# Split operands written as all even tokens and then all odd ones: the order of the writes in a two-layer decoder trunk on one Trainium2 core

## The chip, the cores and the metric

The kernel runs as one program on one core of one Trainium2 chip. A core has four engines that matter here, each with its own instruction queue: PE (TensorE, matrix products), DVE (VectorE), ACT (ScalarE) and POOL (GpSimd). DMA queues move data between the chip's main memory (HBM) and the core's working memory (SBUF); matmuls write into an accumulator memory (PSUM), from which DVE and ACT read. The metric is the time of one execution in microseconds on the device. It was 2062.76 us before the change (median of three runs, 2061.18 to 2065.05).

## The reference: what is computed

Two layers of a decoder trunk for 256 tokens of width 2048, with 16 learned tokens ahead of them (272 in all), everything in float32:

```python
def reference(x, meta_tokens, ...):
    h = jnp.concatenate([meta, x], axis=1)
    for layer in range(DEPTH):                       # 2
        xn = rmsnorm(h, norm_mix[layer])
        if layer < N_A_LAYERS:                       # layer 0: gated linear attention
            h = h + gla_mixer(xn, ...)
        else:                                        # layer 1: windowed attention with sinks
            h = h + swa_mixer(xn, k_sh, v_sh, ...)
        h = h + sq_relu_mlp(rmsnorm(h, norm_mlp[layer]), w_mlp_up[layer], w_mlp_down[layer])
        if layer == N_A_LAYERS - 1:
            k_sh, v_sh = shared_kv(h, kv_norm, w_kv, pos)
    return rmsnorm(h[:, N_META:], norm_final)

def sq_relu_mlp(xn, w_up, w_down):
    return jnp.square(jax.nn.relu(xn @ w_up)) @ w_down
...
```

The MLPs go from 2048 to 8192 and back, and are most of the arithmetic. In the gated attention the mixer's result is scaled by its norm and by `silu(g)` before the output projection; in the windowed attention 32 query heads read 4 shared key and value heads in a band of 128 tokens.

## The kernel before

**Layout.** The stream `h` stays in SBUF, transposed: 16 tiles of 128 rows (the width) by 272 tokens. Every product takes a block of 128 x 128 weights as the stationary operand and streams tokens past it; 16 such blocks are summed in PSUM for one tile of the result. Weights come from HBM in pieces of 512 KB by the queue of SyncE.

**Split operands.** The products are wanted at more precision than PE's fast float32 format (`float32r`) has, so each operand is split into a high part in that format and a low part, the rest. A product is then three matmuls: high weights by high tokens, high weights by low tokens, low weights by high tokens. Weights are split by `split_weight`: ACT makes the high part (L89), DVE the low part (L91). Token operands are kept in the class `Split`: one tile of 2n words for n tokens, in which the order in memory is even tokens' high parts, even tokens' low parts, odd tokens' high parts, odd tokens' low parts. So each part is two rows of n/2 words: 136 for the 272 tokens, 128 for the 256 without the learned ones.

**How matmuls read it.** `x.hi` and `x.lo` are views in the order of the tokens: token 0 from the even row, token 1 from the odd row, token 2 from the even row again. The two neighbours lie n words apart. Where a result for both parts fits into 512 columns of PSUM (256 tokens), one matmul reads both (L114) and a second one reads the high part (L115); for 272 tokens, and where `apart` is false, there are three matmuls (L118, L119, L120).

**Who writes it.** Four places write token operands, each first the high part on ACT and then the low part on DVE, which reads the high part back:

- `split_x` (L161 ACT, L162 DVE): the stream times a norm's gain, 16 tiles each for the gated attention, both MLPs, keys and values, and queries. Beside many of these, POOL adds up the squares for the next norm (`Square.add`).
- the gated output (L700 ACT, L701 DVE): 16 tiles `y` from `gt`, which L697 makes.
- the MLP's hidden tiles (L730 ACT, L731 DVE): 16 tiles in each of 4 blocks of the two layers, 128 in all.
- the windowed attention's outputs, written into the tile `O` straight from PSUM: `values` (L899 ACT, L900 DVE), 8 times, 480 elements for two tiles of 120 + 120 tokens, and `last_values` (L932 ACT, L933 DVE), twice, for the last 16 tokens of a pair of heads.

Their sources are plain: tokens one behind the other. Before the change the producers walk in the order of the tokens. They read neighbours, and write alternately into the two rows, n words apart (256 words in `O`, a tile of its own with rows of 128).

**What sets the order.** Each engine works its own queue in order. In the opening stage the orders of PE, ACT and DVE are written out by hand, and in the windowed attention and its output projection the order of PE is (`manual_schedule`). Everywhere else a planner orders the instructions of each engine when the program is built; it plays the program through with expected durations (L1069):

```python
    with tile.TileContext(nc, schedule_with_timeline_sim=True) as tc:
        trunk(tc, aps, out)
```

**The stages around which the change lies.** (1) The opening, 0 to about 20 us: loads arrive one by one, x is split tile by tile, and the first products run on parts of the weights (L280, L288, L290; their weights are split by L299 and L300). (2) The gated attention, with the masked decays of six levels (L530 to L538), in which every level s works on groups of s tokens of every 2s. (3) The gated output, about 220 to 338 us: `mix` for each of four heads, whose norm is computed by `Square.rstd` (L188 and L189 split the sum of squares, L190 and L191 add it up over the rows on PE, L197 to L204 make the factor), between the products for the gate. (4) The output projection and the first MLP, to about 1135 us. (5) Keys and values, with queries' x split beside it (L796, L806), to about 1160 us. (6) The windowed attention, to about 1330 us: products for the queries with scores (L874), softmax (L829 to L846), transposes (L885 to L887) and values (L896) of earlier steps between them. (7) Its output projection, the second MLP and the last norm (L987 to L995).

Of the kernel before, what the change touches and what calls it, by code (L numbers as in the profile page):

```python
# [11 lines left out]
F32 = mybir.dt.float32  # L12
F32R = mybir.dt.float32r
I32 = mybir.dt.int32
AF = mybir.ActivationFunctionType
ALU = mybir.AluOpType
# [3 lines left out]
P = 128  # L20
# [25 lines left out]
GRP = QH // KVH  # L46
# [18 lines left out]
def trunk(ctx: ExitStack, tc: tile.TileContext, a: dict, out: bass.AP):  # L65
    nc = tc.nc
# [27 lines left out]
    def pairs_of(t):  # L94

        return t.rearrange("p (j a) -> p j a", a=2)

    class Split:


        def __init__(self, tile_, n):
            self.n, self.both = n, tile_[:, :2 * n].rearrange("p (a s j) -> p s j a", a=2, s=2)
            self.hi, self.lo = self.both[:, 0], self.both[:, 1]

    def passes(ps, hi, lo, xs, first, last, m=P, apart=True):

# [50 lines left out]

    def split_x(src, scale_col):
        x = Split(xp.tile([P, 2 * L], F32R, tag="x", name="x"), src.shape[-1])
        src = pairs_of(src)  # L160
        nc.scalar.activation(x.hi, src, AF.Copy, scale=scale_col)  # L161
        nc.vector.scalar_tensor_tensor(x.lo, src, scale_col, x.hi.bitcast(F32), ALU.mult, ALU.subtract)  # L162
        return x

    class Square:
# [57 lines left out]
    with ExitStack() as gla:  # L223
# [41 lines left out]
        def take(k0, k1):  # L265
            for k in range(k0, k1):
                xs.append(split_x(h[k], gains[:, 0, k:k + 1]))
# [54 lines left out]
        with tc.manual_schedule(engines={mybir.EngineType.PE, mybir.EngineType.Activation, mybir.EngineType.DVE}):  # L322
# [3 lines left out]
            for u in range(2):  # L326
                for m in range(NF):
# [4 lines left out]
                    part = m % 2  # L332
# [63 lines left out]
        with tc.issue_after(scaled_keys.ins):  # L396
            for m in range(NF, 8):
                ps, = product(a["w_in"][8 + m], xs, begun=w5 if m == NF else None, pool=aux if m == NF else acc)
# [22 lines left out]
        for m in range(8):  # L421
            log_gate(m)
            ps, = product(a["w_in"][m], xs)
# [11 lines left out]
        with tc.issue_after(rank_done.ins):  # L435
            for li, s in enumerate(LEVELS):
                n = P // (2 * s)
# [246 lines left out]
        for m in range(KT):  # L684
            g, mm = divmod(m, 4)
            if mm == 0:
                mix(g)
            ps, = product(a["w_in"][32 + m], xs)
            gt = tp.tile([P, L], F32, tag="t1", bufs=4, name="gt")
            nc.vector.tensor_mul(gt, ps, rs)  # L690
            sg = tp.tile([P, L], F32, tag="t2", bufs=4, name="sg")
            nc.gpsimd.tensor_scalar_max(sg, gt, -80.0)
            nc.scalar.activation(sg, sg, AF.Exp, scale=-1.0)
            nc.scalar.activation(sg, sg, AF.Ln, bias=1.0)
            nc.scalar.activation(sg, sg, AF.Exp, scale=-1.0)
            nc.vector.tensor_mul(gt, gt, sg)
            nc.vector.scalar_tensor_tensor(gt, OT[g][:, mm], no[:, mm:mm + 1], gt, ALU.mult, ALU.mult)  # L697
            y = Split(yp.tile([P, 2 * L], F32R, tag="y", bufs=KT, name="y"), L)
            gt = pairs_of(gt)
            nc.scalar.copy(y.hi, gt)  # L700
            nc.vector.tensor_sub(y.lo, gt, y.hi.bitcast(F32))  # L701
            ys.append(y)

        xs, sq = [], Square()
# [9 lines left out]
    def mlp(layer, xs, sq, cols, finish):  # L714
        n = cols.stop - cols.start
        rs = sq.rstd(D, "rs", split=True)
        with tc.tile_pool(name="hid", bufs=KT) as hp, tc.tile_pool(name="wp2", bufs=1) as wp2:
            for b in range(NB):
                hs = []
                for m in range(KT):  # L720
                    if b == 0 and m == 4:
                        pools.append(wp2)
                    ps = total(product(a[f"w_up{layer}"][b * KT + m], xs))
                    u = tp.tile([P, L], F32, tag="t1", bufs=4, name="u")[:, :n]
                    nc.vector.scalar_tensor_tensor(u, ps, 0.0, rs, ALU.max, ALU.mult)
                    u2 = tp.tile([P, L], F32, tag="t2", bufs=4, name="u2")[:, :n]
                    nc.scalar.square(u2, u)
                    y = Split(hp.tile([P, 2 * L], F32R, tag="hid", name="hid"), n)
                    u2 = pairs_of(u2)
                    nc.scalar.copy(y.hi, u2)  # L730
                    nc.vector.tensor_sub(y.lo, u2, y.hi.bitcast(F32))  # L731
                    hs.append(y)
                for m in range(KT):
                    ending = layer == 1 and b == NB - 1 and m == KT - 1
                    for term in product(a[f"w_down{layer}"][b * KT + m], hs, apart=not ending):
                        nc.vector.tensor_add(h[m][:, cols], h[m][:, cols], term)
                    if b == NB - 1:
                        finish(m)
            pools.remove(wp2)
# [3 lines left out]
    def to_kv(m):  # L743
        xk.append(split_x(h[m], gains[:, 2, m:m + 1]))
        sq1.add(h[m])

    mlp(0, xs, sq, slice(0, L), to_kv)


    X = slice(NM, L)  # L750
    rs1 = sq1.rstd(D, "rs", split=True)
    with ExitStack() as swa:
# [37 lines left out]
        for i in range(2):  # L790
            for m in range(4):
# [5 lines left out]
                ps = kv[m][:, :L]  # L797
# [4 lines left out]
                else:  # L802
                    t = tp.tile([P, L], F32, tag="t1", bufs=4, name="vt")
# [14 lines left out]
        O = ap.tile([P, KT, 2, 2, SEQ // 2], F32R, name="O")  # L818

        def attended(part, ms, tokens):  # L820

            return O[:, ms, :, part, tokens.start // 2:tokens.stop // 2].rearrange("p m a j -> p m j a")
        N1, N3 = P - NM, NM
        N2 = N1 + P

# [24 lines left out]
        class Step:  # L850
# [39 lines left out]
            def values(self):  # L890
                PT, m0 = self.PT, self.m0
                ps = acc.tile([P, 512], F32, tag="acc", name="ps_pv")
                pv = ps[:, :2 * N2].rearrange("p (i q) -> p i q", i=2)
                for t, q, begin, end in ((0, slice(0, N1), True, True), (1, slice(N1, N2), True, False), (2, slice(N1, N2), False, True)):
                    for par, kv in enumerate(HALVES):
                        nc.tensor.matmul(pv[kv, :, q], VT[t // 2][:, self.pair, kv], PT[t][:, 2 * par:2 * par + 2, :q.stop - q.start], start=begin, stop=end)  # L896
                oh, ol = (attended(part, slice(m0, m0 + 2), slice(0, N2)) for part in range(2))
                pv = pv.rearrange("p i (j a) -> p i j a", a=2)
                nc.scalar.copy(oh, pv)  # L899
                nc.vector.tensor_sub(ol, pv, oh.bitcast(F32))  # L900

# [22 lines left out]
            def last_values(self):  # L924
                ps = aux.tile([P, 512], F32, tag="aux", name="ps_pv3")
                for b, nb in enumerate((P, P, NM)):
                    for t, kv in zip(self.PT3, HALVES):
                        nc.tensor.matmul(ps[kv, :P], VT[b][:nb, self.pair, kv], t[:nb, b], start=(b == 0), stop=(b == 2))
                ms = slice(self.pair * GRP, (self.pair + 1) * GRP)
                src = ps[:, :P].rearrange("p (i j a) -> p i j a", i=GRP, a=2)  # L930
                oh, ol = (attended(part, ms, slice(N2, SEQ)) for part in range(2))
                nc.scalar.copy(oh, src)  # L932
                nc.vector.tensor_sub(ol, src, oh.bitcast(F32))  # L933
# [8 lines left out]
        with tc.manual_schedule(engines={mybir.EngineType.PE}):  # L942
            steps = []
            for t in range(2 * GRP // 2):
                pair, j = divmod(t, GRP // 2)
# [46 lines left out]
    for k0, k1 in ((0, 1), (1, 3), (3, 6), (6, 10), (10, 14), (14, KT)):  # L992
        t = scaled[:, k0:k1]
# [80 lines left out]
```

## Time and profile before

One execution was profiled. Its own time was 2060.31 us, and the profile's span is 2058.6 us.

| | |
|---|---|
| median of three runs | 2062.76 us |
| the three runs | 2061.18, 2062.76, 2065.05 us |
| the profiled execution's own time | 2060.31 us |
| its span | 2058.6 us |
| mean granted clock of PE | 0.997 |
| HBM read over the span | 376.82 MB, 184 GB/s with what is written |

How to read the lines. The page gives for each engine its busy time, its share of the span and its count of instructions. PEld is the loading of weights, which overlaps with PE. A row of a group names the line, the engine, the operation, result and sources, their shapes, the count, the busy time in us and the mean duration in ns; behind the bar stands how long the engine had been idle just before, and what ended most of that. Matmuls are pipelined, so each lasts longer (0.28 us for 272 columns) than the distance to the next one (0.11 us). On ACT and DVE, too, a next instruction can begin shortly before the one ahead has ended, so the distances of starts are what a queue of them costs. A wait is put down to the instruction that released it last.

The page's chain of work that ended last and its costliest groups, apart from those that the prediction shows, in short: splitting weights takes 740.4 us of ACT (L89, 707 times, 1048 ns) and 872.4 us of DVE (L91, 707 times, 1235 ns); the matmuls of the two MLPs, L114, L115 and L118 to L120, are nearly all of PE.

### The profile page before, as it was taken

How to read it: one execution, taken by the hardware profiler on the slowest of the kernel's cores; microseconds unless marked ns; L12 is line 12 of the kernel's file. 1: busy time of each engine (PE TensorE's matmuls, PEld its weight loads, DVE VectorE, ACT ScalarE, POOL GpSimd, SP SyncE). 2: the span in 40 equal slices, each digit the busy share in tenths (PEclk: the TensorE clock that was granted, in tenths of full speed). 3: DMA queues.
4: the chain of work that ended last, by engine and by line, in shares of the span. 5: the costliest groups of instructions: out<-in, count | busy, mean ns of one | idle time of the engine just before them, and what ended most of it. 6: DMA issues, size and time to landing. Idle time of an engine off the chain costs nothing. (4 is left out here: it accounts for less than half of the span.)

```text
span 2058.6 us, 39099 instructions
## 1 busy us (share of the span) xinstructions
PE 2030.5 (99%) x15978; PEld 1951.3 (95%) x15978; DVE 1404.8 (68%) x1999; ACT 1130.7 (55%) x1729; POOL 202.3 (10%) x209
## 2 busy tenths in 40 slices
PE   9999999999999999999999999999999999999997
PEld 9999999999999999999999988999999999999997
DVE  7799677766556556655667777697666666666776
ACT  7565665455345435534554578756546545644653
POOL 0000233300000000000024111060000000000032
PEclk9999999999999999999999999999999999999999
DMA  7644445565655555555554654466666666666662
GB/s 242 194 160 142 150 144 180 189 230 190 192 188 191 189 192 187 192 188 193 186 190 154 203 161 141 135 229 211 203 199 203 200 201 202 201 200 203 200 200 103
DMA packets 109124, 383.85 MB, mean 186 GB/s; under 512 B 13328, under 2 KB 15888, under 8 KB 108944
## 3 DMA queue, kind: packets, MB, share of 16 engines
q1 hardware_dynamic: 106640, 378.29, 56.9%
q0 software_dynamic: 1152, 2.38, 0.4%
q8 instruction: 125, 2.05, 0.4%
q10 hardware_dynamic: 1152, 0.68, 0.1%
q14 instruction: 55, 0.45, 0.1%
HBM read 376.82 MB, written 2.10 MB: 184 GB/s over the span
## 5 line engine op out<-in xcount | busy, mean ns | idle before, releaser
L91 DVE TENSOR_TENSOR lo<-raw,hi 128x1024 fp32r<-128x1024 f32 x707 | 872.4, 1235 | 468.8 <-ACT hi L89 460.8
L89 ACT CAST hi<-raw 128x1024 fp32r<-128x1024 f32 x707 | 740.4, 1048 | 782.4 <-PE ps L119 435.8
L119 PE MATMUL ps<-x,hi 128*128 128x272 f32 (+1 forms) x2032 | 567.4, 279 | 2.3 <-DVE x L162 2.3
L118 PE MATMUL ps<-x,hi 128*128 128x272 f32 (+1 forms) x2032 | 568.6, 280 | 0.0
L120 PE MATMUL ps<-x,lo 128*128 128x272 f32 (+1 forms) x2032 | 567.6, 280 | 0.3 <-DVE lo L91 0.3
L119 PEld LDWEIGHTS ps<-x,hi 128*128 128x128 f32 x2032 | 385.5, 190 | 2.9 <-DVE x L162 2.7
L118 PEld LDWEIGHTS ps<-x,hi 128*128 128x128 f32 x2032 | 385.5, 190 | 2.6 <-issue 2.1
L120 PEld LDWEIGHTS ps<-x,lo 128*128 128x128 f32 x2032 | 385.3, 190 | 1.1 <-DVE lo L91 0.6
L114 PE MATMUL ps<-x,hi 128*128 128x512 f32 x1024 | 335.9, 382 | 0.0
L114 PE MATMUL ps<-hid,hi 128*128 128x512 f32 x1008 | 330.1, 382 | 0.0
L118 PE MATMUL ps<-hid,hi 128*128 128x272 f32 (+1 forms) x1040 | 290.1, 279 | 0.0
L119 PE MATMUL ps<-hid,hi 128*128 128x272 f32 (+1 forms) x1040 | 290.1, 279 | 0.0
L120 PE MATMUL ps<-hid,lo 128*128 128x272 f32 (+1 forms) x1040 | 290.1, 279 | 0.0
L115 PE MATMUL ps<-x,lo 128*128 128x256 f32 x1024 | 279.2, 273 | 0.0
L115 PE MATMUL ps<-hid,lo 128*128 128x256 f32 x1008 | 274.1, 273 | 0.0
L114 PEld LDWEIGHTS ps<-x,hi 128*128 128x128 f32 x1024 | 193.5, 189 | 27.0 <-DVE x L162 0.2
L114 PEld LDWEIGHTS ps<-hid,hi 128*128 128x128 f32 x1008 | 190.2, 189 | 26.4
L115 PEld LDWEIGHTS ps<-x,lo 128*128 128x128 f32 x1024 | 196.6, 192 | 0.3 <-DVE lo L91 0.3
L118 PEld LDWEIGHTS ps<-hid,hi 128*128 128x128 f32 x1040 | 196.6, 189 | 0.0
L119 PEld LDWEIGHTS ps<-hid,hi 128*128 128x128 f32 x1040 | 196.6, 189 | 0.0
L120 PEld LDWEIGHTS ps<-hid,lo 128*128 128x128 f32 x1040 | 196.6, 189 | 0.0
L115 PEld LDWEIGHTS ps<-hid,lo 128*128 128x128 f32 x1008 | 193.5, 192 | 0.2
(259 smaller groups left out, 2214.0 us busy)
## 6 DMA issues: line engine op xcount, KB each, us to landing
raw<-in_w_up SPq DMA_DIRECT2D x256, 512.0 KB, 4.2
raw<-in_w_down SPq DMA_DIRECT2D x256, 512.0 KB, 4.2
raw<-in_w_in SPq DMA_DIRECT2D x91, 512.0 KB, 3.4
raw<-in_w_out_a SPq DMA_DIRECT2D x32, 512.0 KB, 4.0
raw<-in_w_q SPq DMA_DIRECT2D x32, 512.0 KB, 3.6
raw<-in_w_out_b SPq DMA_DIRECT2D x32, 512.0 KB, 3.4
raw<-in_w_kv SPq DMA_DIRECT2D x8, 512.0 KB, 3.5
sw<-qt POOLq DMA_DIRECT2D x32, 64.0 KB, 4.3
```

The lines of the kernel that those rows point to most:

```text
L89: nc.scalar.copy(hi, raw)
L91: nc.vector.tensor_sub(lo, raw, hi.bitcast(F32))
L114: nc.tensor.matmul(both, wh, x.both, start=begin, stop=False)
L115: nc.tensor.matmul(both[:, 1], wl, x.hi, start=False, stop=end)
L118: nc.tensor.matmul(out, wh, x.hi, start=begin, stop=False)
L119: nc.tensor.matmul(out, wh, x.lo, start=False, stop=False)
L120: nc.tensor.matmul(out, wl, x.hi, start=False, stop=end)
```

## The change

The producers visit the elements in another order: all even tokens, then all odd ones. Each then writes its part as two rows without a gap (136 or 128 words; 120 in `values`, 8 in `last_values`), and reads its source at every second element. `Split` gets two more views, `hi_runs` and `lo_runs`, with the tokens' parity outside; a new helper `runs_of` gives the source in the same order. The low part's read of the high part goes along the same rows. The views `hi`, `lo` and `both`, which the matmuls use, and the tile's layout stay as they were. The weights' splitting is not touched.

```diff
+    def runs_of(t):
+
+        return t.rearrange("p (j a) -> p a j", a=2)
...
         def __init__(self, tile_, n):
             self.n, self.both = n, tile_[:, :2 * n].rearrange("p (a s j) -> p s j a", a=2, s=2)
             self.hi, self.lo = self.both[:, 0], self.both[:, 1]
+            runs = tile_[:, :2 * n].rearrange("p (a s j) -> p s a j", a=2, s=2)
+            self.hi_runs, self.lo_runs = runs[:, 0], runs[:, 1]
...
     def split_x(src, scale_col):
         x = Split(xp.tile([P, 2 * L], F32R, tag="x", name="x"), src.shape[-1])
-        src = pairs_of(src)
-        nc.scalar.activation(x.hi, src, AF.Copy, scale=scale_col)
-        nc.vector.scalar_tensor_tensor(x.lo, src, scale_col, x.hi.bitcast(F32), ALU.mult, ALU.subtract)
+        src = runs_of(src)
+        nc.scalar.activation(x.hi_runs, src, AF.Copy, scale=scale_col)
+        nc.vector.scalar_tensor_tensor(x.lo_runs, src, scale_col, x.hi_runs.bitcast(F32), ALU.mult, ALU.subtract)
...
-            gt = pairs_of(gt)
-            nc.scalar.copy(y.hi, gt)
-            nc.vector.tensor_sub(y.lo, gt, y.hi.bitcast(F32))
+            gt = runs_of(gt)
+            nc.scalar.copy(y.hi_runs, gt)
+            nc.vector.tensor_sub(y.lo_runs, gt, y.hi_runs.bitcast(F32))
...
-                    u2 = pairs_of(u2)
-                    nc.scalar.copy(y.hi, u2)
-                    nc.vector.tensor_sub(y.lo, u2, y.hi.bitcast(F32))
+                    u2 = runs_of(u2)
+                    nc.scalar.copy(y.hi_runs, u2)
+                    nc.vector.tensor_sub(y.lo_runs, u2, y.hi_runs.bitcast(F32))
...
         def attended(part, ms, tokens):
 
-            return O[:, ms, :, part, tokens.start // 2:tokens.stop // 2].rearrange("p m a j -> p m j a")
+            return O[:, ms, :, part, tokens.start // 2:tokens.stop // 2]
...
-                pv = pv.rearrange("p i (j a) -> p i j a", a=2)
+                pv = pv.rearrange("p i (j a) -> p i a j", a=2)
                 nc.scalar.copy(oh, pv)
                 nc.vector.tensor_sub(ol, pv, oh.bitcast(F32))
...
-                src = ps[:, :P].rearrange("p (i j a) -> p i j a", i=GRP, a=2)
+                src = ps[:, :P].rearrange("p (i j a) -> p i a j", i=GRP, a=2)
```

## The prediction, made before the changed kernel was run

> **What bounds the kernel now.** I read the page first, then busy time in stretches of 20 us, then the waits of PE.
>
> ```profile
> span 2058.6 us, 39099 instructions
> PE 2030.5 (99%) x15978; PEld 1951.3 (95%) x15978; DVE 1404.8 (68%) x1999; ACT 1130.7 (55%) x1729; POOL 202.3 (10%) x209
> ```
>
> PE is busy for 2030.5 of 2058.6 us. DVE and ACT, on which the whole change lies, have room in the mean, so their own time is worth nothing except where PE waits for them. Does their writing slow PE down in another way, as when both use the memory at once? Two stretches of the first MLP answer that: one of the up projection, where split operands are written, and one of the down projection, where none is.
>
> ```profile
> 600.00:620.00 20.00, 20.00 (x175) 20.00 (x174) 12.53 (x16) 11.41 (x15) 0.00 (x0) 1.00 0.59 187
> 720.00:740.00 20.00, 20.00 (x175) 20.00 (x174) 10.20 (x11) 7.75 (x8) 0.00 (x0) 1.00 0.55 185
> ```
>
> Both hold 175 matmuls. The writes cost PE nothing there, so the 128 pairs of L730 and L731, the greatest part of the change, can bring nothing to the end. What is left is PE's waits:
>
> ```profile
> PE ps_ssq L190 <- ACT sqh L188: 3.7, 2, 1.9
> PE ps L119 <- DVE x L162: 2.3, 2, 1.3
> PE ps_pv L896 <- ACT PT L887: 1.7, 2, 1.5
> PE s L874 <- DVE O L933: 1.4, 1, 1.4
> PE ps L119 <- DVE y L701: 0.9, 1, 0.9
> PE pt L885 <- DVE mx L829: 0.8, 1, 0.8
> PE ps L118 <- ACT y L700: 0.6, 1, 0.6
> PE ps_pv L928 <- ACT PT L920: 0.6, 1, 0.6
> ```
>
> These add up to 12.0 us, and that is all that faster producers could reach, but for one thing: after some waits PE's clock falls. The last three numbers of these rows are granted clock, DMA share and GB/s.
>
> ```profile
> 280.00:300.00 20.00, 20.00 (x155) 19.83 (x155) 14.95 (x25) 11.81 (x20) 6.22 (x3) 0.92 0.50 160
> 300.00:320.00 20.00, 18.26 (x156) 18.00 (x156) 14.05 (x24) 12.61 (x27) 6.96 (x6) 1.00 0.42 134
> 1220.00:1240.00 20.00, 18.29 (x146) 15.60 (x144) 14.04 (x40) 16.54 (x51) 3.87 (x8) 0.91 0.39 123
> ```
>
> 0.08 and 0.09 of 20 us are 1.6 and 1.8 us lost: a dip of the clock costs about 1.7 us, and this execution has two. The first follows the longest wait (L190, 1.9 us), the second the wait at L896 (1.5). The other wait at L190 (3.7 less 1.9, so 1.8 us, in the stretch from 300) is followed by none. So a wait of this size may or may not bring a dip.
>
> **What each producer costs, before and after.** The change alters no count and no destination: the same 15978 matmuls read the same addresses. Only the order in which ACT and DVE visit the elements changes. Now the writes jump by n words at every element; afterwards they run on, and one source is read at every second word.
>
> ```profile
> L730 ACT CAST hid<-u 128x272 fp32r<-128x272 f32 x64 | 43.8, 685 | 2.0
> L188 ACT CAST sqh<-ssq 128x272 fp32r<-128x272 f32 x6 | 2.5, 417 | 3.4 <-POOL ssq L179 3.4
> L161 ACT ACTIVATE x<-h,gains 128x272 fp32r<-128x272 f32 x48 | 35.5, 775 | 1.4 <-DMA gains<-in_gains 0.6 <-DMA h<-in_h 0.5 <-DVE h L151 0.3
> L988 ACT ACTIVATE scaled<-h,gains 128x256 f32<-128x256 f32 x16 | 8.2, 510 | 2.7 <-DVE h L736 2.5
> L731 DVE TENSOR_TENSOR hid<-u,hid 128x272 fp32r<-128x272 f32 x64 | 40.2, 630 | 0.0
> L189 DVE TENSOR_TENSOR sql<-ssq,sqh 128x272 fp32r<-128x272 f32 x6 | 2.6, 438 | 1.7 <-ACT sqh L188 1.7
> ```
>
> L188 and L189 do what L730 and L731 do, with everything in line: 417 for 685 ns on ACT, 438 for 630 on DVE. For L161 the like is L988, 510 for 775. What does a read at every second word cost? The gated attention has it: the last level of L532 and of L535 (s=1) takes every second element.
>
> ```profile
> L535 DVE TENSOR_TENSOR W<-E,K x12: 678/691/705, 114.0 to 188.5; 128x512 f32<-128x512 f32 x12
> L532 ACT ACTIVATE E<-E x12: 629/634/707, 113.0 to 185.5; 128x512 f32<-128x512 f32 x12
> ```
>
> No L535 is above 705 ns (median 691), although at s=1 all its three operands step by two: at most 14 ns on DVE. On ACT the dearest is 73 ns above the median for 512 elements, 39 for 272. So I take **0.19 us** saved on DVE (630 - 438) and **0.22** on ACT (685 - 417 - 39, rounded down; the same for L161). The bounds are 0 (the step is as dear as the jump) and 0.19 and 0.27. [...]
>
> The attention's outputs come from PSUM, and no row reads PSUM at a step.
>
> ```profile
> L899 ACT CAST O<-ps_pv 128x480 fp32r<-128x480 f32 x8 | 8.2, 1028 | 0.9 <-PE ps_pv L896 0.9
> L900 DVE TENSOR_TENSOR O<-ps_pv,O 128x480 fp32r<-128x480 f32 x8 | 8.2, 1027 | 0.9 <-ACT O L899 0.9
> L887 ACT COPY PT<-pt 128x512 f32<-128x512 f32 x24 | 12.7, 585 | 0.0
> L515 DVE TENSOR_TENSOR AT<-ps_d,ident 128x512 f32<-128x512 f32 x2 | 1.4, 692 | 0.0
> ```
>
> With everything in line they would fall to about 0.58 and 0.67; with a step as dear as the jump they stay at 1.03. The nearest row is the instruction itself (same source, same size, one stream out of line), so I take **nothing** saved here and keep 0.44 (ACT) and 0.36 (DVE) for the range. [...]
>
> **Where that reaches PE.** In the gated output stage:
>
> ```profile
> 277.43 0.66 ACT L700 CAST y<-gt 128x272 fp32r<-128x272 f32 x1 [1.51 <-DVE gt L697]
> 277.90 0.42 ACT L188 CAST sqh<-ssq 128x272 fp32r<-128x272 f32 x1
> 335.58 0.66 ACT L700 CAST y<-gt 128x272 fp32r<-128x272 f32 x1 [1.85 <-DVE gt L697]
> 336.27 0.64 DVE L701 TENSOR_TENSOR y<-gt,y 128x272 fp32r<-128x272 f32 x1 [0.72 <-ACT y L700]
> 336.97 0.38 PE L119 MATMUL ps<-y,hi 128*128 128x272 f32 x1
> ```
>
> L188, for which PE waits, stands right behind an L700 on ACT; 0.22 off L700 is 0.22 off the wait, and the second such wait has the same order with one L89 between: 0.44. Then the last y: PE waits for L700 and next for L701, 0.22 + 0.19 = 0.41. Together **0.85**. Behind these waits stand the norm's POOL sums and L697, unchanged, so no more comes out.
>
> In the K/V stage the last x come late on DVE:
>
> ```profile
> 1156.42 1.16 DVE L162 SCALAR_TENSOR_TENSOR x<-h,qgains,x 128x256 fp32r<-128x256 f32 x2
> 1157.41 1.22 DVE L91 TENSOR_TENSOR lo<-raw,hi 128x1024 fp32r<-128x1024 f32 x1
> 1158.55 0.66 DVE L162 SCALAR_TENSOR_TENSOR x<-h,qgains,x 128x256 fp32r<-128x256 f32 x1
> 1159.26 0.38 PE L119 MATMUL ps<-x,hi 128*128 128x256 f32 x1 [1.02 <-DVE x L162]
> ```
>
> Three L162 lie in this line before PE starts again: 3 x 0.19 = **0.57**. DVE's start there is set by a DMA for the rotation, which does not move. At the start of the program:
>
> ```profile
> PEld ps L288 <- DVE lo L300: 0.3, 1, 0.3
> ```
>
> Up to four L162 stand before that L300; I take **0.2** of the 0.3 (0 if a load is late next).
>
> In the attention five L900 lie on the chain; the first and the last:
>
> ```profile
> 1216.04 0.95 DVE O L900
> 1301.94 0.94 DVE O L900
> ```
>
> If they fell by 0.36 each, one would be taken off the wait at L896 and one off that at L928 (0.72), one and the small L933 behind it off that at L874 (0.46), and the last two with an L899 ahead would take away the whole 0.8 at L885: 2.0. With nothing saved on them, it is 0, which I take.
>
> **Sum:** 0.85 + 0.57 + 0.2 = 1.6 us, with both dips as they are. The profiled run took 2060.31 us (1.7 around its span); it becomes 2058.7. It lies 2.45 below the median of the three runs, 2062.76, which becomes **2061.2**; the own range of this case is 2060.2 to 2062.8. A measurement of this kernel can tell about 0.2%, 4.1 us, from no change; so I expect no change that can be told.
>
> **Rivals.** (a) A dip goes: a wait that now brings one is shortened by 0.2 us and stays below what brings it. 1.6 + 1.7 = 3.3, 2059.5; both gone, 5.0, 2057.8. For it: a wait of 1.8 us brought none. Against: 0.2 is little. (b) PSUM at a step is cheap: 1.6 + 2.0 = 3.6, 2059.2, and with a dip gone too 2057.5. For it: L535. Against: PSUM is another memory. (c) The step costs what the jump did and the change moves nothing: 2062.8. Against: L535 and L532. (d) The other side: outside the hand-written stretches a planner orders the work by durations that it expects, and shorter producers may make it choose another order, one in which PE meets a norm's matmul (as L190) before its sum is there. Each such wait costs 1.9 us and a dip of 1.7, 3.6; one gives 2064.8, two give 2068.4, and two are needed for a slowdown that can be told. For it: L190's two waits show that the present order has such places. Against: the attention's PE order is written by hand, and in the MLPs, most of the span, any order keeps PE full.
>
> **Chances.** The forecast 0.35; (a) with one dip 0.22, with both 0.08; (b) 0.20, half of it with a dip; (c) 0.06; (d) 0.09, of which 0.07 beyond 4.1 us. Below 2058.6 are (a) with both dips, (b) with a dip, and 0.04 for scatter of the rest: faster 0.22. Slower 0.07. Same 0.71. The range leaves out the lowest of (a) and (b) and the second step of (d): 2056.5 to 2065.0.
>
> **What would show it.** L730 near 0.46 us and L731 near 0.44; L161 near 0.55; L162 without POOL beside it 0.19 shorter; DVE's and ACT's busy time lower by tens of us with PE's the same; the waits L190, L119 at x and y shorter by 0.2 to 0.6. L899 and L900 at 1.03 confirm the choice, at 0.6 and 0.7 rival (b). Stretches with the clock below 1.00 count the dips. I am wrong if L731 stays at 0.63, or if PE waits at places where it does not now.

## The result and the profile after

| | before | after |
|---|---|---|
| median | 2063.91 us (4 runs, 2061.18 to 2065.08: the three from before and one more) | 2049.73 us (4 runs, 2049.36 to 2050.28) |
| profiled execution | 2060.31 us, span 2058.6 | 2049.36 us, span 2047.6 |

The ratio is 0.9933, with a 95% interval from 0.9916 to 0.9951: about 14 us (10 to 17) off. A second series gave 2050.24 us (5 runs) and 0.9941 [0.9929, 0.9953], about 12 us off. The prediction, 2061.2 us in a range from 2056.5 to 2065.0, missed it.

Every engine issues the same instructions in the same order as before, so all of it is timing. The lines of the changed kernel that matter here lie 6 further down: L118 to L120 are L124 to L126 now, L161 and L162 are L167 and L168, L188 and L190 are L194 and L196, L690 to L701 are L696 to L707, L730 and L731 are L736 and L737, L896 to L900 are L902 to L906, and L933 is L939. All experiments but one (named there) have the changed kernel's line numbers.

The page of the kernel after, its span and busy times:

```profile
span 2047.6 us, 39099 instructions
PE 2025.3 (99%) x15978; PEld 1948.6 (95%) x15978; DVE 1367.4 (67%) x1999; ACT 1088.2 (53%) x1729; POOL 193.7 (9%) x209
```

DVE is busy 37.4 us less and ACT 42.5, "lower by tens of us" as the prediction had it. But the span fell by 11.0 us, and POOL, none of whose instructions was touched, is busy 8.6 us less; 5.3 of these are the maximum over `gt` (L692, 26.7 us before, 21.4 after). The groups of instructions, with shapes kept apart:

```profile
L736 ACT CAST hid<-u 128x256 fp32r<-128x256 f32 x64 | 33.0, 518 | 2.0
L737 DVE TENSOR_TENSOR hid<-u,hid 128x256 fp32r<-128x256 f32 x64 | 30.7, 481 | 0.0
L736 ACT CAST hid<-u 128x272 fp32r<-128x272 f32 x64 | 29.0, 454 | 2.0
L737 DVE TENSOR_TENSOR hid<-u,hid 128x272 fp32r<-128x272 f32 x64 | 27.7, 434 | 0.0
L906 DVE TENSOR_TENSOR O<-ps_pv,O 128x480 fp32r<-128x480 f32 x8 | 5.2, 650 | 0.0
L905 ACT CAST O<-ps_pv 128x480 fp32r<-128x480 f32 x8 | 4.5, 558 | 1.4 <-PE ps_pv L902 1.4
```

For 272 tokens L736 fell from 685 to 454 ns and L737 from 630 to 434: 0.23 and 0.20 us, near the prediction's 0.22 and 0.19. The two reads of PSUM, for which it took nothing, fell from 1028 to 558 and from 1027 to 650. What PE waits for in the kernel after:

```profile
PE ps_ssq L196 <- ACT sqh L194: 1.3, 1, 1.3
PE s L880 <- DVE O L939: 1.0, 1, 1.0
PE ps L125 <- DVE x L168: 0.9, 1, 0.9
PE ps_pv L902 <- ACT PT L893: 0.8, 1, 0.8
PE s L912 <- POOL qs L871: 0.7, 1, 0.7
PE ps L125 <- DVE y L707: 0.7, 1, 0.7
PE ps_pv L934 <- ACT PT L926: 0.6, 1, 0.6
PE ps L124 <- ACT y L706: 0.5, 1, 0.5
```

One of two waits for `sqh` is gone (3.7 us in all became 1.3), one of two for `x` (2.3 to 0.9), one of two for `PT` (1.7 to 0.8). And busy time in stretches of 20 us, where the last three numbers are granted clock, DMA share and GB/s:

```profile
260.00:280.00 20.00, 20.00 (x168) 19.78 (x167) 15.30 (x25) 14.73 (x30) 5.03 (x6) 1.00 0.52 167
280.00:300.00 20.00, 20.00 (x167) 19.78 (x167) 13.28 (x22) 11.64 (x25) 7.00 (x5) 1.00 0.52 177
300.00:320.00 20.00, 18.67 (x161) 18.47 (x160) 15.86 (x27) 10.92 (x20) 6.09 (x5) 1.00 0.40 132
1220.00:1240.00 20.00, 19.30 (x168) 16.69 (x167) 14.20 (x43) 16.36 (x50) 2.53 (x6) 1.00 0.42 136
```

The stretch from 280 us holds 167 matmuls at clock 1.00; before it held 155 at 0.92. Neither of the two dips of the clock is left. Stage by stage (bounds are starts of the same instructions, of keys and values from the first copy of a key tile on; PE's standing time and the loss to the clock are summed over stretches of 0.5 us):

| stage | before | after | PE stands | lost to the clock |
|---|---|---|---|---|
| opening and gated attention | 219.9 | 219.9 | 3.8, 3.8 | 0, 0 |
| gated output | 118.4 | 112.8 | 5.9, 2.6 | 1.7, 0 |
| output projection, first MLP | 806.2 | 805.4 | 0, 0 | 0, 0 |
| keys and values | 16.1 | 14.9 | 2.4, 0.9 | 0, 0 |
| windowed attention | 166.0 | 163.0 | 4.7, 3.2 | 1.7, 0 |
| rest | 732.0 | 731.6 | 11.6, 11.6 | (only behind PE's last work) |

So of 11.0 us, about 6 are standing time, 3.4 the two dips, and some 1.6 lie in differences too small to place.

### The profile page after: what moved, and what is told of

It is laid out like the page before. It is cut to its first block, busy times and chain, and to the rows that moved or that the text cites. A ratio compares the mean times of both kernels' runs of the same rounds, so it can differ in the third digit from the quotient of the medians.

```text
span 2047.6 us, 39099 instructions
## 1 busy us (share of the span) xinstructions
PE 2025.3 (99%) x15978; PEld 1948.6 (95%) x15978; DVE 1367.4 (67%) x1999; ACT 1088.2 (53%) x1729; POOL 193.7 (9%) x209
## 3 DMA queue, kind: packets, MB, share of 16 engines
q0 software_dynamic: 1152, 2.38, 0.4%
## 5 line engine op out<-in xcount | busy, mean ns | idle before, releaser
L91 DVE TENSOR_TENSOR lo<-raw,hi 128x1024 fp32r<-128x1024 f32 x707 | 872.6, 1235 | 502.6 <-ACT hi L89 495.4
L124 PE MATMUL ps<-x,hi 128*128 128x272 f32 (+1 forms) x2032 | 567.8, 279 | 0.0
L126 PE MATMUL ps<-x,lo 128*128 128x272 f32 (+1 forms) x2032 | 566.7, 279 | 0.0
L124 PEld LDWEIGHTS ps<-x,hi 128*128 128x128 f32 x2032 | 384.8, 189 | 2.5 <-issue 2.3
L126 PEld LDWEIGHTS ps<-x,lo 128*128 128x128 f32 x2032 | 384.6, 189 | 0.5
L120 PE MATMUL ps<-x,hi 128*128 128x512 f32 x1024 | 335.7, 382 | 0.0
L120 PE MATMUL ps<-hid,hi 128*128 128x512 f32 x1008 | 330.1, 382 | 0.0
L124 PE MATMUL ps<-hid,hi 128*128 128x272 f32 (+1 forms) x1040 | 290.1, 279 | 0.0
L126 PE MATMUL ps<-hid,lo 128*128 128x272 f32 (+1 forms) x1040 | 290.1, 279 | 0.0
L120 PEld LDWEIGHTS ps<-x,hi 128*128 128x128 f32 x1024 | 193.5, 189 | 27.0
L120 PEld LDWEIGHTS ps<-hid,hi 128*128 128x128 f32 x1008 | 190.2, 189 | 26.3
L124 PEld LDWEIGHTS ps<-hid,hi 128*128 128x128 f32 x1040 | 196.6, 189 | 0.0
L126 PEld LDWEIGHTS ps<-hid,lo 128*128 128x128 f32 x1040 | 196.6, 189 | 0.0
```

What stands on the lines that cost most here:

```text
L91: nc.vector.tensor_sub(lo, raw, hi.bitcast(F32))
L120: nc.tensor.matmul(both, wh, x.both, start=begin, stop=False)
L124: nc.tensor.matmul(out, wh, x.hi, start=begin, stop=False)
L126: nc.tensor.matmul(out, wl, x.hi, start=False, stop=end)
```

## The experiments

Unless said otherwise, a ratio is to the kernel before run on the same chip, whose medians were 2061.9 to 2062.8 us.

### Which producer brings it

Four kernels are the kernel before with one of the four kinds of producer in runs and the others in pairs, for example for the gated output:

```diff
-            gt = pairs_of(gt)
-            nc.scalar.copy(y.hi, gt)
-            nc.vector.tensor_sub(y.lo, gt, y.hi.bitcast(F32))
+            gt = runs_of(gt)
+            nc.scalar.copy(y.hi_runs, gt)
+            nc.vector.tensor_sub(y.lo_runs, gt, y.hi_runs.bitcast(F32))
```

> Only the gated output (ACT hi and DVE lo of y) is written in runs; everything else as before. Theory (the gain comes by stage: in the gated output the shorter producers take away the wait for the sum of squares, POOL's collisions and the clock's dip behind it): the stretch from the first ps_o matmul to the first residual add, 118.5 us before and 112.9 after the whole change, becomes 112.9 to 114; everything else within 0.5 us; total 4 to 6 us below the kernel before. Rival (the gain comes from the mass of producers, the 128 hidden tiles, by less contention everywhere): total within 1 us of before. Rival (only the direct chain counts, as in the prediction): 0.85 us.

> Only split_x is written in runs. Theory: the stretch from the first residual add to the first copy of a query tile, 822.3 us before and 820.3 after, becomes about 820.5, because PE's two waits for x in the K/V stage (2.3 us) fall to 0.9 or less; the attention behind it may shift by a dip of the clock (1.7 us) either way; total 1.5 to 3.5 us below before. Rival (mass of producers): under 1 us.

> Only the attention's outputs O are written in runs, read from PSUM at every second element. Theory: ACT's copy falls from 1028 to about 558 ns and DVE's subtraction from 1027 to about 650, and the stretch from the first query copy to the last ps_pv matmul, 165.9 us before and 162.9 after, becomes 162 to 164; total 2 to 4 us below before. Rival (mass): under 0.5 us. Rival (the dip of the clock alone is what the attention gained, by luck of phase): the waits of PE keep their 4.5 us and only the stretch with clock 0.5 goes.

> Only the 128 hidden tiles of the MLPs are written in runs, which is most of what the change frees on ACT (some 25 us) and DVE (some 21 us). Theory (PE hides them all): total within 0.5 us of before, apart from dips of the clock elsewhere. Rival (mass of producers, contention): most of the 11 to 14 us.

| in runs | median | ratio | to before (2062.7) | stage that changes |
|---|---|---|---|---|
| gated output `y` | 2056.97 | 0.9971 [0.9958, 0.9983] | -5.7 | gated output 112.9 |
| `x` | 2059.78 | 0.9987 [0.9978, 0.9996] | -2.9 | keys and values 15.0 |
| `O` | 2060.06 | 0.9985 [0.9975, 0.9994] | -2.6 | windowed attention 164.8 |
| hidden tiles | 2062.22 | 0.9998 [0.9989, 1.0008] | -0.5 | none |

The four add up to 11.7 us, near the whole. In the profiles the stage of `y` fell by 5.5 us, near its 5.7 (a dip of 1.7 us in the profile of before is among them); the stages of `x` and `O` fell by 1.1 and 1.2 us, less than the 2.9 and 2.6 of the medians, and where the rest of these lies was not found. The 128 hidden tiles, the greatest part of the change, bring nothing that can be told, while 16 tiles of `y` bring nearly half.

### The gated output: VectorE's part or ScalarE's

The kernel before, with only one of the two instructions that write `y` in runs (`runs` and `pairs` are the two views of `gt`):

```diff
-            nc.scalar.copy(y.hi, gt)
-            nc.vector.tensor_sub(y.lo, gt, y.hi.bitcast(F32))
+            nc.scalar.copy(y.hi, pairs)
+            nc.vector.tensor_sub(y.lo_runs, runs, y.hi_runs.bitcast(F32))
```

and the other way round.

> Before, with only VectorE's part of the gated tiles' split (the difference into y) written in runs; ScalarE's copy keeps its pairs. Theory A (a shorter VectorE instruction leaves gaps in which POOL's maximum over gt is not held up): the gated stage falls from 118.4 us to 113 to 114.5 us, PE's longest wait for sqh from 1.9 to 1.3 us or less, time 2057 to 2059 us. Rival B (ScalarE's queue is what was late, and its shorter copy is what helped): the stage stays at 117 to 118.5 us, the time at 2062 to 2064 us.

> Before, with only ScalarE's part of the gated tiles' split (the copy into y) written in runs; VectorE's difference keeps its pairs. Theory A: the gated stage stays at 117 to 118.5 us and POOL's maximum keeps its median of 1.8 us; 2062 to 2064 us. Rival B: the stage falls to 113 to 114.5 us and the time to 2057 to 2059 us, with POOL's maximum as slow as before.

VectorE's part alone: 2059.61 us, 0.9989 [0.9981, 0.9998]. ScalarE's alone: 2062.47 us, 1.0002 [0.9993, 1.0011]. The groups of POOL's maximum, in the kernel before, with VectorE's part and then with ScalarE's:

```profile
L692 POOL TENSOR_SCALAR sg<-gt 128x272 f32<-128x272 f32 x16 | 26.7, 1667 | 65.9 <-DVE gt L690 65.9
```

```profile
L698 POOL TENSOR_SCALAR sg<-gt 128x272 f32<-128x272 f32 x16 | 24.2, 1512 | 65.5 <-DVE gt L696 65.5
```

```profile
L698 POOL TENSOR_SCALAR sg<-gt 128x272 f32<-128x272 f32 x16 | 27.1, 1693 | 65.4 <-DVE gt L696 65.4
```

The rival falls: ScalarE's shorter copy alone brings nothing, and its POOL time is near that of before. Theory A holds in kind but not in size: VectorE's part alone brought 3.1 us, the stage came to 115.5 us, not to 113 to 114.5, and the time lies above the 2057 to 2059 of the theory; one wait for `sqh` went, the other stayed, longer (2.9 us). Only both parts together bring the 5.7.

### What POOL has to do with it

POOL's maximum over `gt` (L692 before, L698 after) stands in the chain of every gate: VectorE makes `gt`, POOL takes the maximum with -80, ScalarE three functions, VectorE two products, ScalarE the copy into `y`. The view of that line, in the kernel before:

```profile
L692 POOL TENSOR_SCALAR sg<-gt x16: 887/1789/2634, 226.9 to 329.7; 128x272 f32<-128x272 f32 x16
...
  ACT sg L693: 23.0, 13
```

and of the kernel after:

```profile
L698 POOL TENSOR_SCALAR sg<-gt x16: 885/1040/2559, 226.8 to 324.4; 128x272 f32<-128x272 f32 x16
...
  ACT sg L699: 14.9, 10
```

These are the least, the median and the greatest duration in ns, and what ScalarE waited for it. The same instruction takes mostly 0.89 to 1.07, 1.79 or about 2.6 us; before the change 5 of the 16 are short (1.07 us or less), after it 10. The timeline of one that changed, before:

```profile
242.34 0.49 DVE L697 SCALAR_TENSOR_TENSOR gt<-OT,norm_out,gt 128x272 f32<-128x272 f32 x1
242.50 2.63 POOL L692 TENSOR_SCALAR sg<-gt 128x272 f32<-128x272 f32 x1 [3.84 <-DVE gt L690]
242.75 1.22 DVE L91 TENSOR_TENSOR lo<-raw,hi 128x1024 fp32r<-128x1024 f32 x1
243.88 0.63 DVE L701 TENSOR_TENSOR y<-gt,y 128x272 fp32r<-128x272 f32 x1
245.16 0.43 ACT L693 ACTIVATE sg<-sg 128x272 f32<-128x272 f32 x1 [1.40 <-POOL sg L692]
```

and after:

```profile
242.04 0.49 DVE L703 SCALAR_TENSOR_TENSOR gt<-OT,norm_out,gt 128x272 f32<-128x272 f32 x1
242.21 1.07 POOL L698 TENSOR_SCALAR sg<-gt 128x272 f32<-128x272 f32 x1 [3.62 <-DVE gt L696]
242.48 1.40 DVE L91 TENSOR_TENSOR lo<-raw,hi 128x1024 fp32r<-128x1024 f32 x1
243.31 0.43 ACT L699 ACTIVATE sg<-sg 128x272 f32<-128x272 f32 x1
243.81 0.43 DVE L707 TENSOR_TENSOR y<-gt,y 128x272 fp32r<-128x272 f32 x1
```

Before, POOL's 2.63 us are the 0.89 of the shortest of the 16 and 1.74 more, and the two VectorE instructions beside it, one right behind the other, last from 242.75 to 244.51, which is 1.76. After, POOL gets through first, and L91 is the one that is held up (1.40 instead of 1.22). So the maximum and VectorE's instructions hold each other up here, POOL by 1.74 us in the first trace and L91 by 0.18 in the second; by what means, no trace shows. In both traces POOL started first, 0.25 and 0.27 us ahead of L91, while L697 (L703 after) was still running; what decided this pair was not found.

For most of the others the order of the starts decides. In the two profiles L91 had started 0.16 to 0.18 us ahead of the maximum 14 times, and these took 1.79 to 2.21 us; in 6 cases L91 started after it and no VectorE instruction ran at its start, and these took 0.89. Four maxima passed from the first kind to the second, such as this one, before and after:

```profile
252.37 1.22 DVE L91 TENSOR_TENSOR lo<-raw,hi 128x1024 fp32r<-128x1024 f32 x1
252.55 1.79 POOL L692 TENSOR_SCALAR sg<-gt 128x272 f32<-128x272 f32 x1 [2.98 <-DVE gt L690]
```

```profile
250.74 0.89 POOL L698 TENSOR_SCALAR sg<-gt 128x272 f32<-128x272 f32 x1 [3.04 <-DVE gt L696]
251.17 1.23 DVE L91 TENSOR_TENSOR lo<-raw,hi 128x1024 fp32r<-128x1024 f32 x1 [0.52 <-ACT hi L89]
```

In all four, L91 came right behind L690 before the change, and after it had to wait (0.17 to 0.52 us) for ScalarE's `hi`, so that POOL was ahead: VectorE, done sooner with the earlier work, had reached L690 before ScalarE had that `hi` ready. It fits that ScalarE's shorter copy alone brought nothing: it lets `hi` come sooner, too.

That the gain lies here and not in VectorE's and ScalarE's own shorter time shows gate by gate, from one start of L690 (L696) to the next. In the five steps whose maximum became shorter by 0.9 us or more (5.2 us together) the step lost 4.5 us, one dip of the clock among them; in the ten others, where the writes became shorter as much, it lost 0.8 in all.

To test it, the maximum goes to VectorE, in the kernel before (no other edit) and in the kernel after:

```diff
-            nc.gpsimd.tensor_scalar_max(sg, gt, -80.0)
+            nc.vector.tensor_scalar_max(sg, gt, -80.0)
```

The planner then moves a few instructions of this stage on PE, VectorE and ScalarE, so here the order is not quite the same.

> Before, all writes in pairs, with the maximum of gt with -80 on VectorE in place of POOL; the planner then moves a few instructions of the gated stage on PE, VectorE and ScalarE. Theory A (POOL's 0.9 to 2.6 us in the chain of the gate are what PE's wait for sqh came from): the gated stage falls from 118.4 us to 111 to 114 us, without a stretch at half clock in it, and the time to 2056 to 2059 us. Rival B (POOL has slack): the stage stays within 1 us of 118.4, the time at 2062 to 2065 us, since VectorE does 16 instructions more.

> After, with the maximum of gt with -80 on VectorE in place of POOL. Theory A: what is left of the wait for sqh (1.3 us once) falls under 0.7 us, the gated stage from 112.8 to 111 to 112 us, the time to 2047.5 to 2049 us. Rival B: within 0.7 us of the changed kernel's 2049.7 us; if VectorE becomes what is late in the stage, 2050 to 2052 us.

The kernel before with it: 2053.84 us, 0.9962 [0.9949, 0.9974]. The kernel after with it: 2047.07 us, 0.9928 [0.9915, 0.9942]. In both the gated output takes 106.5 us and PE does not stand in it at all (2 to 3 us come back in the stages up to the queries). The group in the kernel before with the edit:

```profile
L698 DVE TENSOR_SCALAR sg<-gt 128x272 f32<-128x272 f32 x16 | 4.8, 298 | 0.2
```

0.30 us on VectorE replace 0.89 to 2.63 on POOL. Theory A holds, by more than it had said: without one write in another order, this edit brings 9 us (5 to 11 by the interval). Part of that is the shorter instruction itself, and part may be the planner's other order; the runs do not separate them. Then the other way, the maximum twice on POOL in the kernel after:

```diff
             nc.gpsimd.tensor_scalar_max(sg, gt, -80.0)
+            nc.gpsimd.tensor_scalar_max(sg, sg, -80.0)
```

> After, with the maximum of gt with -80 taken twice on POOL (the second in place, the result unchanged). Theory (the POOL instruction stands in the chain that PE waits for, and stretches at half clock follow PE's waits): the gated stage grows from 112.8 to 115 to 120 us, PE's waits for sqh from 1.3 to 3 to 6 us, time 2052.5 to 2058 us, and the mean granted clock of the runs falls from 0.998 to 0.996 to 0.997. Rival (POOL has slack after the change, the gain came from VectorE's and ScalarE's own time): 2049.7 us within 0.7 us, clock 0.998.

It took 2053.42 us (2052.50 to 2055.06), 3.2 to 3.7 above the kernel after's two medians (other series). Two rows of its waits and groups:

```profile
PE ps_ssq L196 <- ACT sqh L194: 3.6, 2, 2.2
```

```profile
L698 POOL TENSOR_SCALAR sg<-gt 128x272 f32<-128x272 f32 x16 | 20.9, 1304 | 52.3 <-DVE gt L696 45.0 <-ACT hi L89 7.3
L698 POOL TENSOR_SCALAR sg<-sg 128x272 f32<-128x272 f32 x16 | 20.2, 1261 | 1.3
```

The stage grew to 116.0 us and the second wait for `sqh` came back, as the theory said. The clock hardly followed: 0.997 in three of six runs and 0.998 in the others, where 0.996 to 0.997 was expected.

### Keys and values

The kernel before, with the splits of `x` in runs only for 256 tokens (queries and second MLP), or only for 272:

```diff
-        src = pairs_of(src)
+        xh, xl, src = (x.hi_runs, x.lo_runs, runs_of(src)) if src.shape[-1] < L else (x.hi, x.lo, pairs_of(src))
```

> Before, with only the 256-token splits of x (for the queries of attention, and for the second MLP) written in runs. Theory (the splits that stand among the K/V stage's work on ScalarE and VectorE delay the weight splits, the rotation's multiply and so the x that PE waits for): the K/V stage falls from 16.1 us to about 15.0 us, VectorE's wait for the rotation's DMA from 1.8 to about 1.0 us, PE's waits for x from 2.3 to about 0.9 us, time 2059 to 2061 us. Rival (the 272-token splits at the end of the first MLP are late): all of it stays as before, 2062 to 2064 us.

> Before, with only the 272-token splits of x (opening, end of the gated stage, end of the first MLP) written in runs. Theory: K/V stage at 16.1 us, PE's waits for x at 2.3 us, time 2062 to 2064 us. Rival: K/V stage about 15.0 us, waits for x about 0.9 us, 2059 to 2061 us.

For 256 tokens: 2059.95 us, 0.9986 [0.9977, 0.9995], PE's waits for `x` 1.4 us, the stage 15.6 us. For 272: 2061.44 us, 0.9997 [0.9988, 1.0006], waits 2.3 us, the stage 16.2. So it is the splits among the stage's own work that count. For the queries' 256 tokens VectorE's L162 fell from 754 to 485 ns with the whole change, 0.27 us and not 0.19. But the 256-token ones alone did not bring VectorE's wait for the rotation to 1.0 us; it was 1.6. The timeline's row for it, before and after the whole change:

```profile
1155.78 0.72 DVE L775 TENSOR_TENSOR sw<-sw,sin 128x544 f32<-128x544 f32 x1 [1.79 <-DMA sw<-kt]
```

```profile
1148.55 0.73 DVE L781 TENSOR_TENSOR sw<-sw,sin 128x544 f32<-128x544 f32 x1 [0.91 <-DMA sw<-kt]
```

From issue to landing these DMAs took 6.5 us before, 5.0 after, 4.7 with all of `x` in runs, 6.0 and 6.6 with 256 and 272 tokens alone. So a transfer that no edit touches became shorter. Why, is open: they go by POOL's queue (q0 on the page, 2.38 MB), not by the weights' (q1), and no run changed what else goes on at the time.

### The attention's reads of PSUM

The kernel before, with only ScalarE's copies into `O` in runs, or only VectorE's differences:

```diff
-                nc.vector.tensor_sub(ol, pv, oh.bitcast(F32))
+                nc.vector.tensor_sub(*(t.rearrange("p m a j -> p m j a") for t in (ol, pv, oh.bitcast(F32))))
```

> Before, with only ScalarE's copies from PSUM into O in runs; VectorE's differences keep their pairs. Theory A (ScalarE's copy, 1028 to about 560 ns, stands ahead of the probabilities that PE's second matmuls wait for): PE's wait for them falls from 1.5 to about 0.8 us, the wait for O (VectorE) stays at 1.4 us, time 2060.5 to 2062 us. Theory B (VectorE's difference, 1027 to about 650 ns, is the one that counts): no wait but that for O changes, 2062 to 2063.5 us.

> Before, with only VectorE's differences from PSUM into O in runs; ScalarE's copies keep their pairs. Theory A: the wait for the probabilities stays at 1.5 us, the wait for O falls from 1.4 to about 1.0 us, time 2061.5 to 2063 us. Theory B: both waits fall as in the changed kernel, 2059.5 to 2061 us.

ScalarE's part: 2061.37 us, 0.9996 [0.9986, 1.0005]. VectorE's: 2060.00 us, 0.9989 [0.9980, 0.9998]. PE's waits with ScalarE's part, then with VectorE's:

```profile
PE ps_pv L902 <- ACT PT L893: 1.8, 2, 1.5
PE s L880 <- DVE O L939: 1.4, 1, 1.4
```

```profile
PE s L880 <- DVE O L939: 1.0, 1, 1.0
PE ps_pv L902 <- ACT PT L893: 1.4, 1, 1.4
```

Neither theory holds as put. The wait for `O` is VectorE's, as theory A said. The wait for `PT` did not fall with ScalarE's copies, as A wanted, and hardly with VectorE's, as B wanted. With all of `O` in runs it was 0.8 us, but in the profile of the kernel after from the second series it was 1.5 again (0.8 in the first), so it differs between executions of one kernel and decides nothing here. By the times, VectorE's part brings most; how the rest of the stage's 3.0 us divides is open.

### Rows at another distance

L736 and L737 are dearer for 256 tokens than for 272 (518 and 481 ns against 454 and 434), though they do less. In the kernel after, the rows of 128 words were laid 136 apart, so that the two rows that one instruction writes (with a row of the other part between them) start 272 words apart and not 256 (its lines lie one further down):

```diff
-            self.n, self.both = n, tile_[:, :2 * n].rearrange("p (a s j) -> p s j a", a=2, s=2)
+            v = tile_.rearrange("p (a s j) -> p a s j", a=2, s=2)[:, :, :, :n // 2]
+            self.n, self.both = n, v.rearrange("p a s j -> p s j a")
```

> After, with the rows of 256-token splits laid out at the 136-word distance of the 272-token ones (the rows keep 128 words). Theory on the sizes (rows that follow each other at 128 words cost more, not the shorter row itself): the hidden tiles' VectorE difference of the second MLP goes from 481 to about 430 ns and ScalarE's copy from 518 to about 440 ns. Rival: both stay within 15 ns. On the time both say the same, since these tiles are hidden behind PE: 2049.7 us within 1 us.

```profile
L737 ACT CAST hid<-u 128x256 fp32r<-128x256 f32 x64 | 28.0, 440 | 2.0
L738 DVE TENSOR_TENSOR hid<-u,hid 128x256 fp32r<-128x256 f32 x64 | 26.7, 419 | 0.0
```

518 became 440 ns and 481 became 419: the distance was what cost. The time was 2051.10 us, 0.9942 [0.9929, 0.9954], the same ratio as the kernel after's second series; 1.4 us above its first median, a little outside what was expected. Its granted clock was 0.997 in three of five runs, and its profile has a dip of 3.4 us at half clock behind a wait of 1.0 us at 1258 us: dips can come back although the waits are as in the kernel after.

### More runs, and a faster kernel

The kernel after was run again, and with it a kernel in which VectorE has both small POOL instructions that PE's waits lead to: the maximum, and the copy into `qs` (L871).

```diff
-                    nc.gpsimd.tensor_copy(self.qs[:, 2 * self.j * N3:2 * (self.j + 1) * N3].rearrange("p (i q) -> p i q", i=2), self.QR[:, :, N2:])
+                    nc.vector.tensor_copy(self.qs[:, 2 * self.j * N3:2 * (self.j + 1) * N3].rearrange("p (i q) -> p i q", i=2), self.QR[:, :, N2:])
```

> After, with both small POOL instructions that PE waits behind moved to VectorE: the maximum of gt with -80, and the copy of 128x32 queries into qs. Theory (a POOL instruction is stretched where it meets VectorE's; the one copy of 1.14 us among seven of 0.21 us is such a case): PE's wait of 0.7 us for qs goes, 0.3 to 0.8 us less than with the maximum alone: 2046.2 to 2046.8 us. Rival (VectorE in order is later there): within 0.3 us of 2047.1 us or above it.

> The changed kernel as it is, in more runs. Theory (its waits are too short to bring stretches at half clock, so that its runs scatter less than those of before, 2055.9 to 2066.4 us): median 2049 to 2050.5 us, all runs within 2 us, granted clock 0.998 in nearly all. Rival (its four runs were lucky): a scatter of 5 us or more and clocks of 0.994 to 0.997, median 2051 to 2054 us.

> The changed kernel with both small POOL instructions on VectorE, beside the changed kernel on the same chip. Theory: 2.5 to 3.5 us less than the changed kernel, since PE does not stand in the gated stage at all. Rival (the difference seen in separate series is one between chips): within 1 us of it.

The kernel after: 2050.24 us (2049.66 to 2051.20), all five at a granted clock of 0.998. With the two moves: 2046.80 us in the first series (0.9923 [0.9910, 0.9935], the upper end of what was expected), and 2046.23 us (2045.22 to 2046.94), 0.9922 [0.9908, 0.9935], in the second, on the same chip as the kernel after: 4.0 us below it, more than the 2.5 to 3.5 expected. L871 in the kernel after and with the moves:

```profile
L871 POOL COPY qs<-QR x8: 210/211/1142, 1167.1 to 1274.5; 128x32 f32<-128x32 f32 x8
...
  PE s L912: 0.7, 1
```

```profile
L871 DVE COPY qs<-QR x8: 173/178/182, 1165.8 to 1271.9; 128x32 f32<-128x32 f32 x8
```

On POOL the same small copy took 0.21 us seven times and 1.14 once; on VectorE it takes 0.18. But the long one is not the one that PE waited for. It ran here, 0.14 us behind the start of an L91 (1191.27, 1.22 us):

```profile
1191.41 1.14 POOL L871 COPY qs<-QR 128x32 f32<-128x32 f32 x1 [5.99 <-DVE QR L782]
...
1225.41 0.21 POOL L871 COPY qs<-QR 128x32 f32<-128x32 f32 x1 [8.20 <-DVE QR L782]
```

PE's first matmul that reads `qs` started at 1225.76, behind the second row, a short copy that came late because VectorE's L782 did. With the moves that wait went, and one of 0.3 to 0.4 us for the softmax's maximum on VectorE came in its place; so the theory's reason, a stretched copy, is not what PE waited for. Both series lie within 0.9 us of the maximum alone (2047.07 us, another series), so what the second move adds cannot be told.

## Why the prediction was wrong, step by step

**Right: where the change cannot matter.** The hidden tiles bring nothing (0.9998), PE's work is unchanged, and the order of the instructions stayed, so rival (d) did not come. **Right: the sizes on SBUF.** A write in line and a read at a step of two save 0.20 us on VectorE and 0.23 on ScalarE for 272 tokens. For 256 tokens the rows' distance takes part of it back (481 and 518 ns; 419 and 440 with the rows 136 words apart).

**Failed: PSUM.** "The nearest row is the instruction itself ..., so I take **nothing** saved here." 0.47 and 0.38 us were saved: the instructions, which now read PSUM at a step of two, take 558 and 650 ns, not more than the 0.58 and 0.67 us that the prediction gave for everything in line. This was rival (b), whose 2.0 us are near the 2.6 that `O` alone brought (1.2 in the stage of its profile). The jump in the rows of before lay in the write, and the row that mixed it with the read was no evidence for the read.

**Failed, and the largest: the gated output.** 0.85 us were counted, "Behind these waits stand the norm's POOL sums and L697, unchanged, so no more comes out." `y` alone brought 5.7. The terms were counted on the last two links of the chain only. Further back in the same chain stood POOL's maximum, an instruction that the change does not touch but whose duration, 0.9 to 2.6 us, depends on what VectorE does beside it, and on which of the two starts first. An unchanged instruction was taken for one of unchanged cost. Its spread of durations stood in the trace of before.

**Failed: "a DMA for the rotation, which does not move".** It landed 1.5 us sooner after its issue. And the three L162 were priced at 0.19 us each where 0.27 was saved. The 0.57 us forecast for keys and values became 1.2 in the stage.

**Failed: "with both dips as they are".** Both went, 3.4 us. Rival (a) had that for 0.08, worked out for waits shortened by 0.2 us; in the gated output the wait itself was gone. In the attention a wait of 1.5 us came without a dip in the second series' profile; so for a single execution chance has a part; nine of nine runs at a clock of 0.998 (next point) are hardly chance, though which wait brings a dip was not found.

**Failed: the step from the profiled run to the median.** 2.45 us were added to carry the result over, as if they were a constant of the kernel. They go with the clock: among 100 runs of the kernel before, in the five series of experiments, the 12 with a granted clock of 0.998 took 2060.0 us in the mean and the 16 with 0.994 took 2064.9. All nine runs of the changed kernel have 0.998 and lie between 2049.4 and 2051.2, so at equal clock some 10 us are left: the waits are the larger part. The waits differ between executions, too: the second wait for `sqh` was 1.7 us in the profiles of before, `x`, `O` and VectorE's part of `O`, and 2.9 in those of the hidden tiles, of `x` for 256 or 272 tokens alone and of ScalarE's part of `O`, in all of which this stage is unchanged.

**The opening** brought 0 of the 0.2 forecast.

## What to carry to other kernels

Before an edit to VectorE is priced, look for POOL instructions in the chains that PE waits for, and at the spread of their durations, not their mean: here the spread (0.89 to 2.63 us for one instruction) was worth more than the edit, and moving 16 small instructions off POOL brought 9 us alone (5 to 11). When a chain ends in a wait, follow it back through every engine until an instruction that the change cannot shift, and count a whole wait, with the dip of the clock that may follow it (1.7 us here), as what can be won. Where a duration could come from its read or its write, look for a row that has only one of them before it is taken as evidence for the other.

## What the runs showed of the hardware

- **POOL against VectorE.** The POOL maximum over 128x272 took 0.89 us in the 6 cases in which VectorE's L91 (1.23 to 1.40 us) started behind it, by 0.10 to 0.44 us, and nothing ran on VectorE at its start, 1.79 to 2.21 in the 14 in which L91 had started 0.16 to 0.18 us earlier, and 2.56 and 2.63 in the 3 with L697, L91 and L701 beside it, one behind the other (L703, L91 and L707 after). In the kernel after, the POOL copy of 128x32 took 0.21 us seven times, and 1.14 the one time it started 0.14 us behind an L91.
- **The clock after a wait.** In 19 profiles, from 200 us to shortly before the end, PE stood some 52 times for 1.3 us or more and some 36 times for 0.9 to 1.3 (summed over stretches of 0.5 us, so a few lie on a bound); 15 and 3 of these were followed, within 4 us, by 3.4 us (four times twice as long) at half the clock. No such stretch in that range came without a wait. The waits followed by one lasted about 1.0 to 2.9 us; why these and not the others, no trace shows.
- **PSUM at a step of two** cost ScalarE and VectorE nothing that can be seen: 558 and 650 ns for 480 elements, against 585 and 692 for 512 in line (L887 and L515 before).
- **The distance of two output rows of 128 words** has a price: with rows laid 128 words apart (the two that are written start 256 apart) a split of 256 elements took 518 ns on ScalarE and 481 on VectorE, with 136 (272) it took 440 and 419. Why is not known.
